# A two-block transformer kernel: the downward products of the second block's MLPs by seven products of halves (Strassen's method)

## The chip, the cores and the metric

The kernel runs on one core of one Trainium2 chip. A core has a matrix engine (TensorE, PE in the profile; PEld is its loading of weights), three engines for elementwise work (VectorE = DVE, ScalarE = ACT, GpSimd = POOL), queues that start transfers (here above all that of SyncE, SPq), an on-chip memory SBUF, and PSUM, into which PE writes its sums. Each engine runs its own list of instructions in order, and waits on semaphores for the others. The metric is the time of one execution on the device, in microseconds (us).

## The reference

Two blocks, one after the other, on 512 tokens of width 1024, in 32-bit floats. The first is an attention block with a mixture of 32 experts; the change does not touch it. The second has two layers, each with a mixer and then an MLP, and the MLP is what is changed:

```python
S, D_MODEL, D_FF = 512, 1024, 4096
def second_block(x, positions, attn_norm_w, w_in, hgrn_lower_bounds, w_out, mlp_norm_w, w_up, w_down, final_norm_w):
    ...
    for layer in range(2):
        ...
        x = x + mixed @ w_out[layer]
        h = rms_norm_2(x, mlp_norm_w[layer])
        x = x + jnp.square(jax.nn.relu(h @ w_up[layer])) @ w_down[layer]
    return rms_norm_2(x, final_norm_w)
```

## The kernel before

Every large product is made of matmuls on numbers split in two: `split` (L83) writes a rounded high part on ACT (L85) and the remainder on DVE (L86), and `mm3` (L88) adds three matmuls, high by high, high by low and low by high (L90 to L92). Each matmul takes a 128x128 stationary operand and up to 512 columns, and writes one PSUM bank of 128x512 numbers.

`mlp` (L1756) works through the hidden width 4096 in four quarters, `b` = 0 to 3. A quarter has an upward part and a downward part.

- Upward: `cols_mm` (L1395) for four pieces of 256 hidden columns each. A piece is one load of 1 MB on the SP queue (`wide`, L1356), one split of 128x2048 numbers (`whi`, `wlo`), and 48 matmuls of 512 columns into two banks of `pa`. Each bank goes through relu and square on ACT and DVE into the high and low parts `uh`, `ul` (L1785 to L1788). In quarter 0 two pieces are done together, first for the first half of the tokens and then for the second, since the last rows of the normed input are still being made; these matmuls have 256 columns.
- Downward: `rows_mm` (L1368) twice, for output columns 0 to 511 and 512 to 1023. Each takes two loads and splits, and for each of four tiles of 128 tokens 24 matmuls into one bank. DVE adds the bank to the residual stream `xs` (`add_rows`, L1410).

Loaded weights lie in `raw`, three buffers of 1 MB. The split weights of the upward part rotate through two buffers, those of the downward part through two others (pools `hi5`, `lo5`). A framework builds the program: it takes the order of each engine's list from priorities and dependences, so that instructions need not stand in the order of the code, and it inserts the semaphores. Around the MLP stand `mix_attention` with the last normalisation (`normed`, L1309, whose rows are scaled by DVE in L1327 and transposed by PE in L1338), and the next layer's mixer or the final norm.

Of the kernel before, what the change touches and what calls it, by code (L numbers as in the profile page):

```python
# [10 lines left out]
F32 = mybir.dt.float32  # L11
F32R = mybir.dt.float32r
# [3 lines left out]
AF = mybir.ActivationFunctionType  # L16
OP = mybir.AluOpType
# [4 lines left out]
P = 128  # L22
S = 512
D = 1024
NT = S // P
KD = D // P
# [43 lines left out]
def bcast_rows(ap, n):  # L70
    return bass.AP(tensor=ap.tensor, offset=ap.offset, ap=[[0, P], [1, n]])


class K:
# [65 lines left out]
    def build(self):  # L140
        tc = self.tc
        with ExitStack() as ctx:
            E = ctx.enter_context
            self.cp = E(tc.tile_pool(name="consts", bufs=1))
            self.dr = E(tc.tile_pool(name="dr", bufs=1, space=DRAM))
            self.sm = E(tc.tile_pool(name="small", bufs=2, reuse_waits="tile"))
            self.xs = self.cp.tile([P, NT, D], F32, name="xs")
            self.raw = E(tc.tile_pool(name="rawp", bufs=3, reuse_waits="tile"))
            self.rawx, self.nraw = None, 0
            with tc.tile_pool(name="cq", bufs=1, side="right", reuse_waits="tile") as self.cq:  # L150
                with tc.tile_pool(name="ps", bufs=1, space=PSUM) as self.ps:
                    self.first_block()
                self.hip = E(tc.tile_pool(name="hip", bufs=2, reuse_waits="tile"))
                self.lop = E(tc.tile_pool(name="lop", bufs=2, reuse_waits="tile"))
# [1599 lines left out]


    def mlp(self, layer, hh, hl):  # L1756
        nc, tc, A, sm, xs = self.nc, self.tc, self.A, self.sm, self.xs
        DVE, ACT, PE = nc.vector, nc.scalar, nc.tensor
        up, down = A["w_up_2"][layer], A["w_down_2"][layer]
        with ExitStack() as c:  # L1760
            E = c.enter_context
            dn = [E(tc.tile_pool(name=n, bufs=2 if n == "hi5" else 2, reuse_waits="tile")) for n in ("hi5", "lo5")]
            pd = E(tc.tile_pool(name="pd3", bufs=1, reuse_waits="tile"))
            h = None
            if layer == 0:
                h, after = self.normed(pd, A["attn_norm_w_2"][1:2])
            else:
                fw = pd.tile([P, D], F32, name="wb")
                nc.gpsimd.dma_start(fw, bcast_rows(A["final_norm_w_2"], D))

                def after(t):
                    ss = sm.tile([P, 1], F32, name="s1")
                    o = pd.tile([P, D], F32, name="xo", bufs=3)
                    ACT.activation(o, xs[:, t, :], AF.Square, accum_out=ss)  # L1774
                    rs = self.rsqrt_mean(sm, ss, D, 1)
                    DVE.scalar_tensor_tensor(o, xs[:, t, :], rs, fw, OP.mult, OP.mult)  # L1776
                    nc.sync.dma_start(self.out[t * P:(t + 1) * P, :], o)
            for b in range(4):
                uh = pd.tile([P, KD, S], F32R, name="uh")
                ul = pd.tile([P, KD, S], F32R, name="ul")  # L1780

                def done(q):
                    def f(j, pt):
                        r = pd.tile([P, S], F32, name="r", bufs=2)
                        ACT.activation(r, pt, AF.Relu)  # L1785
                        ACT.activation(uh[:, 2 * q + j, :], r, AF.Square)
                        DVE.tensor_tensor(r, r, r, OP.mult)
                        DVE.tensor_tensor(ul[:, 2 * q + j, :], r, uh[:, 2 * q + j, :].bitcast(F32), OP.subtract)  # L1788
                    return f
                ps = [(1024 * b + 256 * q, done(q)) for q in range(4)]  # L1790
                if b == 0:
                    self.cols_mm(hh, hl, up, ps[:2], 2)
                    ps = ps[2:]
                for p in ps:
                    self.cols_mm(hh, hl, up, [p])
                self.rows_mm(uh, ul, down, 0, self.add_rows(0), 8 * b, pools=dn)
                last = b == 3
                self.rows_mm(uh, ul, down, 512, self.add_rows(512, after if last else None), 8 * b, by_tile=last, pools=dn)
        return h


# [25 lines left out]
```

## Time and profile before

| | before |
|---|---|
| median of three runs | 2971.6 us (2971.32 to 2974.15) |
| the profiled execution, its own time | 2975.91 us |
| its span, first to last instruction | 2974.1 us |
| PE busy | 2828.0 us (95%) |
| DVE busy | 2143.2 us (72%) |
| ACT busy | 1611.0 us (54%) |
| POOL busy | 286.8 us (10%) |
| MLP of the first layer, about | 1948 to 2298 us |
| MLP of the second layer, about | 2615 to 2965 us |

Busy shares are means over stages with different limits. The records of neighbouring matmuls overlap, so PE's busy time is no measure of its speed; the spacing of the starts is. The profile says which engine's instruction ended an idle stretch, as in `[2.03 <-PE pa L92]`.

### The profile page before, as it was taken

What the parts mean: (1) busy time and instruction counts of PE and PEld (TensorE: products, weight loads), DVE (VectorE), ACT (ScalarE), POOL (GpSimd) and SP (SyncE); (2) the same over time, 40 slices, a digit from 0 to 9 for tenths busy, and PEclk for the clock granted to TensorE, in tenths of its full rate; (3) what the DMA queues carried; (4) which work ended last, traced back from release to release, by engine and by line L of the source; (5) the groups of instructions that cost most, each with busy time, mean ns of one, the idle gap of its engine ahead of it and who ended that gap; (6) DMA issues with size and microseconds to landing.
All of it is one profiled execution on the core that took longest, in us unless ns stands there. A gap on an engine that the chain in (4) does not pass through costs nothing. (4 is left out here: it accounts for less than half of the span.)

```text
span 2974.1 us, 36626 instructions
## 1 busy us (share of the span) xinstructions
PE 2828.0 (95%) x14296; PEld 2122.7 (71%) x14296; DVE 2143.2 (72%) x3043; ACT 1611.0 (54%) x1846; POOL 286.8 (10%) x125
## 2 busy tenths in 40 slices
PE   6988969999999999999997999999999999999998
PEld 4645747666666666666664877788888877788887
DVE  5798679999999999999997586654334586654334
ACT  5478747777777777777775225742223225743222
POOL 1002201122222222222200000000000000000000
PEclk8999969999999999999998999999999999999999
DMA  7244259999999999999996112132322112033330
GB/s 257 83 148 159 89 177 334 363 362 362 358 364 361 360 363 362 360 363 361 362 356 237 57 57 88 29 114 99 99 94 76 57 57 88 29 115 98 99 99 29
DMA packets 184645, 589.38 MB, mean 198 GB/s; under 512 B 16923, under 2 KB 63494, under 8 KB 151702
## 3 DMA queue, kind: packets, MB, share of 16 engines
q1 hardware_dynamic: 174088, 556.81, 51.7%
q0 software_dynamic: 8016, 28.05, 3.8%
q10 hardware_dynamic: 2366, 2.14, 0.3%
q8 instruction: 114, 1.87, 0.3%
q14 instruction: 61, 0.50, 0.0%
HBM read 567.13 MB, written 19.84 MB: 197 GB/s over the span
## 5 line engine op out<-in xcount | busy, mean ns | idle before, releaser
L86 DVE TENSOR_TENSOR wlo<-raw,whi 128x2048 fp32r<-128x2048 f32 (+2 forms) x528 | 1162.6, 2216 | 362.2 <-ACT whi L85 361.4
L85 ACT ACTIVATE whi<-raw 128x2048 fp32r<-128x2048 f32 (+2 forms) x528 | 972.4, 1854 | 579.6 <-PE pa L92 325.2
L90 PE MATMUL pa<-hh,whi 128*128 128x512 f32 (+1 forms) x808 | 289.8, 360 | 0.9 <-ACT whi L85 0.9
L1065 PE MATMUL ph<-whi,xh 128*96 128x512 f32 x1024 | 288.9, 399 | 0.0
L91 PE MATMUL pa<-hl,whi 128*128 128x512 f32 (+1 forms) x808 | 288.9, 358 | 0.0
L1065 PE MATMUL ph<-wlo,xh 128*96 128x512 f32 x1024 | 288.9, 400 | 0.0
L92 PE MATMUL pa<-hh,wlo 128*128 128x512 f32 (+1 forms) x808 | 287.7, 358 | 0.2 <-DVE wlo L86 0.2
L1065 PE MATMUL ph<-whi,xl 128*96 128x512 f32 x1024 | 277.8, 392 | 0.0
L1065 PEld LDWEIGHTS ph<-whi,xl 128*96 128x96 f32 x1024 | 164.7, 161 | 71.4
L1065 PEld LDWEIGHTS ph<-whi,xh 128*96 128x96 f32 x1024 | 161.3, 162 | 63.5 <-issue 0.3
L1065 PEld LDWEIGHTS ph<-wlo,xh 128*96 128x96 f32 x1024 | 159.2, 162 | 62.0 <-DVE wlo L86 0.6
L91 PE MATMUL pa<-wlo,uh 128*128 128x512 f32 x512 | 199.3, 389 | 0.0
L92 PE MATMUL pa<-whi,ul 128*128 128x512 f32 x512 | 199.2, 389 | 0.0
L90 PE MATMUL pa<-whi,uh 128*128 128x512 f32 x512 | 199.0, 389 | 0.0
L989 POOL DMA_INDIRECT xg<-h2d,ig x32 | 146.2, 4570 | 468.3 <-issue 381.3
L1065 PE MATMUL py<-wlo,ah 128*96 128x512 f32 x512 | 161.9, 397 | 14.1 <-DVE wlo L86 14.0
L90 PEld LDWEIGHTS pa<-hh,whi 128*128 128x128 f32 x808 | 153.9, 191 | 25.7 <-ACT z L572 1.8
L92 PEld LDWEIGHTS pa<-hh,wlo 128*128 128x128 f32 x808 | 153.5, 190 | 22.3 <-DVE wlo L86 0.6
L91 PEld LDWEIGHTS pa<-hl,whi 128*128 128x128 f32 x808 | 154.0, 191 | 21.5
L1065 PE MATMUL py<-whi,al 128*96 128x512 f32 x512 | 159.6, 393 | 0.6 <-DVE al L86 0.6
L1065 PE MATMUL py<-whi,ah 128*96 128x512 f32 x512 | 160.1, 394 | 0.0
L90 PE MATMUL pa<-whi,hh 128*128 128x512 f32 (+2 forms) x352 | 135.6, 386 | 1.3 <-ACT hh L273 1.3
(430 smaller groups left out, 4446.4 us busy)
## 6 DMA issues: line engine op xcount, KB each, us to landing
raw<-in_w_mlp SPq DMA_DIRECT2D x384, 1024.0 KB
raw<-in_w_up SPq DMA_DIRECT2D x32, 1024.0 KB
raw<-in_w_down SPq DMA_DIRECT2D x32, 1024.0 KB
raw<-in_w_in SPq DMA_DIRECT2D x26, 1024.0 KB
raw<-in_w_ada SPq DMA_DIRECT2D x24, 1024.0 KB
raw<-in_w_out SPq DMA_DIRECT2D x8, 1024.0 KB
raw<-in_w_o SPq DMA_DIRECT2D x4, 1024.0 KB
acc<-g SPq DMA_DIRECT2D x5, 512.0 KB
```

The costliest lines, as they stand in the source:

```text
L85: nc.scalar.activation(hi, src, AF.Copy)
L86: (engine or nc.vector).tensor_tensor(lo, src, hi.bitcast(F32), OP.subtract)
L90: mm(out, lh, rh, start=start, stop=False)
L91: mm(out, lh, rl, start=False, stop=False)
L92: mm(out, ll, rh, start=False, stop=stop)
L989: POOL.indirect_dma_start(out=xg, out_offset=None, in_=self.h2d[:, :], in_offset=bass.IndirectOffsetOnAxis(ap=ig[:, :1], axis=0))
L1065: PE.matmul(out[:, 512 * n:512 * n + 512], x[:, kk, :], w[:, nn * k + n, :], start=False, stop=kk == KD - 1 and q == 2)
```

## The change

In quarters 0 to 2 of each layer the downward part (512 tokens x 1024 hidden x 1024 outputs) is seen as 2x2 halves: tokens in two halves, outputs in two halves, and the hidden width in two halves of four 128-row blocks (even and odd blocks). Instead of eight products of halves there are seven, in the form of Strassen's method with shared sums. A product has 24 matmuls of 512 columns into two banks. In the code's order, with the weights that each takes (w11, w21, w12, w22 are the loaded quarters of the weight, and t2, w12', w11', w21' sums of them):

1. `first[0]` by w11; 2. `first[1]` by w21; 3. slot 5 by t2; 4. slot 4 by w12'; 5. slot 6 by w11'; 6. slot 7 by w22; 7. slot 2 by w21'.

The sums of weights w12' = w12 - w11, t2 = w22 - w12', w11' = t2 - w11 and w21' = t2 - w21 are GpSimd operations of 128x2048 numbers (L1809, L1810, L1869, L1875); the sums of activations are DVE operations of 128x256 (L1827 to L1831) in tile `s`. Splits are made in halves of 128x1024, weights into four rotating quarters of two `whi` and two `wlo` tiles (`halves`), activations into `ah`, `al`. Results that go to two places are collected in `u` and added to `xs` by GpSimd, 128x1024 at a time (`both`, L1862); the others are added by DVE from PSUM (L1857). Quarter 3 stays with eight products, with the split weights in the same rotating quarters.

```diff
...
+        hi, lo = [[p.tile([P, 4, 512], F32R, name=n) for _ in range(2)] for p, n in ((self.hip, "whi"), (self.lop, "wlo"))]
+        turn = [0]
+        def halves(raw):
+            k, n = raw.shape[1:]
+            out = []
+            for g in range(2):
+                q = turn[0] % 4
+                turn[0] += 1
+                v = [t[q // 2][:, q % 2 * 2:q % 2 * 2 + 2, :].rearrange("p a b -> p (a b)").rearrange("p (k n) -> p k n", n=n) for t in (hi, lo)]
+                self.split(v[0], v[1], raw[:, g * k // 2:(g + 1) * k // 2, :])
+                out += [(v[0][:, q, :], v[1][:, q, :]) for q in range(k // 2)]
...
+            s = pd.tile([P, 4, 8, 256], F32, name="s")
+            own = {n: pd.tile([P, 4, 512], F32, name="w" + n) for n in ("12", "22", "11", "21")}
+            def pieces(b):
+                for nm, k, n in (("12", 0, 1), ("11", 0, 0), ("22", 1, 1), ("21", 1, 0)):
+                    src = down[8 * b * P:8 * (b + 1) * P, 512 * n:512 * n + 512].rearrange("(q two p) n -> p two q n", two=2, p=P)
+                    nc.sync.dma_start(own[nm], src[:, k])
+                t2 = self.rawtile()
+                POOL.tensor_tensor(own["12"], own["12"], own["11"], OP.subtract)
+                POOL.tensor_tensor(t2, own["22"], own["12"], OP.subtract)
+                return t2
...
+                def done(q):
+                    def f(j, pt):
+                        r = pd.tile([P, S], F32, name="r", bufs=2)
+                        ACT.activation(r, pt, AF.Relu)
+                        DVE.tensor_tensor(s[:, q, 2 * j:2 * j + 2, :].rearrange("p a b -> p (a b)"), r, r, OP.mult)
+                        v = [s[:, q, n, :] for n in range(8)]
+                        ACT.activation(first[j][0][:, q, :], v[2 * j + 1], AF.Copy)
+                        if j == 0:
+                            DVE.tensor_tensor(v[6], v[1], v[0], OP.subtract)
+                        else:
+                            DVE.tensor_tensor(v[4], v[0], v[2], OP.add)
+                            DVE.tensor_tensor(v[5], v[2], v[6], OP.subtract)
+                            DVE.tensor_tensor(v[7], v[3], v[5], OP.subtract)
+                        DVE.tensor_tensor(first[j][1][:, q, :], v[2 * j + 1], first[j][0][:, q, :].bitcast(F32), OP.subtract)
+                    return f
+                ps = [(1024 * b + 256 * q, done(q)) for q in range(4)]
+                n = 2 if b == 0 else 1
+                upper(ps[:n], n)
+                t2 = pieces(b)
+                for p in ps[n:]:
+                    upper([p])
+                def parts(slot):
+                    ah, al = left()
+                    self.split(ah, al, s[:, :, slot, :])
+                    return ah, al
+                def product(banks, a, w):
+                    w = halves(w)
+                    for q, (wh, wl) in enumerate(w):
+                        for n in range(2):
+                            ns = slice(n * P, (n + 1) * P)
+                            self.mm3(banks[n], a[0][:, q, ns], a[1][:, q, ns], wh, wl, q == 0, q == 3)
+                def add(banks, half, col, op=OP.add):
+                    for n in range(2):
+                        o = xs[:, 2 * half + n, 512 * col:512 * col + 512]
+                        DVE.tensor_tensor(o, o, banks[n], op)
+                def both(u, half, col):
+                    o = xs[:, 2 * half:2 * half + 2, 512 * col:512 * col + 512]
+                    POOL.tensor_tensor(o, o, u, OP.add)
...
+                u = pd.tile([P, 2, 512], F32, name="u")
+                x = banks(self.pb)
+                product(x, first[0], own["11"])
+                POOL.tensor_tensor(own["11"], t2, own["11"], OP.subtract)
+                for n in range(2):
+                    ACT.copy(u[:, n, :], x[n])
+                both(u, 1, 0)
+                y = banks(self.py)
+                product(y, first[1], own["21"])
+                POOL.tensor_tensor(own["21"], t2, own["21"], OP.subtract)
+                add(y, 1, 0)
+                z = banks(self.pa)
+                product(z, parts(5), t2)
+                for n in range(2):
+                    DVE.tensor_tensor(u[:, n, :], u[:, n, :], z[n], OP.add)
+                both(u, 1, 1)
+                y = banks(self.pa)
+                product(y, parts(4), own["12"])
+                add(y, 1, 1)
+                add(y, 0, 1)
+                x = banks(self.pb)
+                product(x, parts(6), own["11"])
+                for n in range(2):
+                    DVE.tensor_tensor(u[:, n, :], u[:, n, :], x[n], OP.add)
+                both(u, 0, 0)
+                both(u, 0, 1)
+                y = banks(self.py)
+                product(y, parts(7), own["22"])
+                add(y, 1, 1)
+                y = banks(self.pa)
+                product(y, parts(2), own["21"])
+                add(y, 0, 0, OP.subtract)
+            for b in range(3):
+                quarter(b)
...
-                if b == 0:
-                    self.cols_mm(hh, hl, up, ps[:2], 2)
-                    ps = ps[2:]
-                for p in ps:
-                    self.cols_mm(hh, hl, up, [p])
-                self.rows_mm(uh, ul, down, 0, self.add_rows(0), 8 * b, pools=dn)
-                last = b == 3
-                self.rows_mm(uh, ul, down, 512, self.add_rows(512, after if last else None), 8 * b, by_tile=last, pools=dn)
+            for q in range(4):
+                upper([(1024 * b + 256 * q, done(q))])
+            for c0 in (0, 512):
+                finish = self.add_rows(c0, after if c0 else None)
+                pts = [self.pa() for _ in range(NT)]
+                w = []
+                for q in range(2):
+                    w += load(down, 8 * b + 4 * q, c0, 512, 4)
+                    for t in range(NT if c0 == 0 or q else 0):
+                        ts_ = slice(t * P, (t + 1) * P)
+                        for k in range(0 if c0 else 4 * q, 4 * q + 4):
+                            self.mm3(pts[t], uh[:, k, ts_], ul[:, k, ts_], w[k][0], w[k][1], k == 0, k == KD - 1)
+                        if q:
+                            finish(t, pts[t])
```

Three places of the engines' lists follow, as the built programs have them; what stands behind a name is the tile's number.

On ACT, at the start of the first layer's MLP of before: `whi` from `raw_16368` is the high part of quarter 0's third upward piece, `r` and `uh` the relu and square of the first two pieces' four banks (`pa_16152` to `pa_16155`).

```order
L1785 ACTIVATE r_16276<-pa_16152 128x512
L1786 ACTIVATE uh_16138<-r_16276 128x512
L85 ACTIVATE whi_16370<-raw_16368 128x2048
L1785 ACTIVATE r_16305<-pa_16153 128x512
L85 ACTIVATE whi_16560<-raw_16558 128x2048
L1786 ACTIVATE uh_16138<-r_16305 128x512
```

The same place of the change, where `raw_16384` is the third upward piece, `raw_16454` the fourth, `pa_16156` the last of the four banks, and `ah` the high part of an activation sum:

```order
L1822 ACTIVATE r_16307<-pa_16154 128x512
L1825 ACTIVATE ah_16139<-s_16132 128x256
L1822 ACTIVATE r_16339<-pa_16155 128x512
L1825 ACTIVATE ah_16137<-s_16132 128x256
L1822 ACTIVATE r_16369<-pa_16156 128x512
L1825 ACTIVATE ah_16139<-s_16132 128x256
L85 ACTIVATE whi_16125<-raw_16384 128x1024 x2
L85 ACTIVATE whi_16126<-raw_16454 128x1024 x2
```

The third piece's split, which stood behind the first bank's output, now stands behind the last bank's.

On DVE of the change, from the last upward output of quarter 0 to the middle of product 4 (`r_16516` is the last bank's relu, `raw_16381` is t2, `al_16595` and `al_16632` belong to products 3 and 4, `w12_16133` holds w12'):

```order
L1823 TENSOR_TENSOR s_16132<-r_16516 128x512
L1829 TENSOR_TENSOR s_16132<-s_16132 128x256
L1830 TENSOR_TENSOR s_16132<-s_16132 128x256
L1832 TENSOR_TENSOR al_16140<-s_16132,ah_16139 128x256
L1831 TENSOR_TENSOR s_16132<-s_16132 128x256
L86 TENSOR_TENSOR wlo_16127<-raw_16381,whi_16125 128x1024
L86 TENSOR_TENSOR al_16595<-s_16132,ah_16594 128x1024
L86 TENSOR_TENSOR al_16632<-s_16132,ah_16631 128x1024
L86 TENSOR_TENSOR wlo_16127<-raw_16381,whi_16125 128x1024
L86 TENSOR_TENSOR wlo_16128<-w12_16133,whi_16126 128x1024
L1857 TENSOR_TENSOR xs_63<-xs_63,py_16559 128x512
```

All but the last row read two SBUF operands; in before DVE had, in the downward part of a quarter, four splits and eight additions from PSUM.

On POOL of the change, from the first sum of quarter 0 to the second sum of quarter 1 (`w11_16135`, `w21_16136` and `w22_16134` are single buffers that each quarter loads again, `u_16524` the collected results; before had no row here):

```order
L1809 TENSOR_TENSOR w12_16133<-w12_16133,w11_16135 128x2048
L1810 TENSOR_TENSOR raw_16381<-w22_16134,w12_16133 128x2048
L1869 TENSOR_TENSOR w11_16135<-raw_16381,w11_16135 128x2048
L1875 TENSOR_TENSOR w21_16136<-raw_16381,w21_16136 128x2048
L1862 TENSOR_TENSOR xs_63<-xs_63,u_16524 128x2x512 x2
L1809 TENSOR_TENSOR w12_16133<-w12_16133,w11_16135 128x2048
L1862 TENSOR_TENSOR xs_63<-xs_63,u_16524 128x2x512 x2
L1810 TENSOR_TENSOR raw_16855<-w22_16134,w12_16133 128x2048
```

The next quarter's first sum stands between the two pairs of additions of this quarter.

## Rows read from the trace of the kernel before

**Rows 1.** The page: the span, and busy time by engine.

```profile
span 2974.1 us, 36626 instructions
PE 2828.0 (95%) x14296; PEld 2122.7 (71%) x14296; DVE 2143.2 (72%) x3043; ACT 1611.0 (54%) x1846; POOL 286.8 (10%) x125
```

**Rows 2.** Windows: both MLPs, and one downward part; us, busy, clock, DMA.

```profile
1948.00:2298.00 350.00, 349.13 (x1641) 292.36 (x1640) 153.26 (x170) 106.97 (x112) 0.00 (x0) 1.00 0.32 103
1994.00:2037.00 43.00, 43.00 (x191) 35.63 (x190) 15.10 (x13) 8.78 (x6) 0.00 (x0) 1.00 0.30 98
...
2615.00:2965.00 350.00, 349.64 (x1632) 292.80 (x1631) 147.89 (x174) 100.63 (x105) 0.00 (x0) 1.00 0.28 91
```

**Rows 3.** Waits of PE in 1950 to 2298: us, times, longest.

```profile
PE pb L1338 <- DVE xn L1327: 0.4, 1, 0.4
```

**Rows 4.** Timeline of DVE, downward part: additions after 12 matmuls each.

```profile
2119.77 0.69 DVE L1415 TENSOR_TENSOR xs<-xs,pa 128x512 f32<-128x512 f32 x1 [0.60 <-PE pa L92]
2122.49 0.69 DVE L1415 TENSOR_TENSOR xs<-xs,pa 128x512 f32<-128x512 f32 x1 [2.03 <-PE pa L92]
2125.21 0.69 DVE L1415 TENSOR_TENSOR xs<-xs,pa 128x512 f32<-128x512 f32 x1 [2.03 <-PE pa L92]
```

**Rows 5.** Groups of DVE by shape, 1950 to 2298: count, busy us, mean ns.

```profile
L86 DVE TENSOR_TENSOR wlo<-raw,whi 128x2048 fp32r<-128x2048 f32 x33 | 75.6, 2292 | 130.4 <-ACT whi L85 130.4
...
L1787 DVE TENSOR_TENSOR r<-r 128x512 f32<-128x512 f32 x32 | 21.9, 688 | 24.2 <-ACT uh L1786 24.2
```

**Rows 6.** Groups of ACT by shape, 1950 to 2298.

```profile
L1785 ACT ACTIVATE r<-pa 128x512 f32<-128x512 f32 x32 | 18.8, 587 | 42.7 <-PE pa L92 42.0 <-DVE ul L1788 0.7
L1325 ACT ACTIVATE xn<-xs 128x1024 f32<-128x1024 f32 x4 | 4.2, 1060 | 5.9 <-DVE xs L1415 5.9
```

**Rows 7.** Timeline of POOL in the second layer's mixer.

```profile
2473.12 1.29 POOL L1558 TENSOR_TENSOR xn<-uu 128x512 f32<-128x512 f32 x1 [9.22 <-DVE gs L1752]
2474.50 1.34 POOL L1559 TENSOR_TENSOR uu<-uu 128x512 f32<-128x512 f32 x1
2475.92 0.74 POOL L1560 TENSOR_TENSOR uu<-xn 128x256 f32<-128x256 f32 x1
2476.61 2.79 POOL L1561 TENSOR_TENSOR uu<-xn 128x256 f32<-128x256 f32 x1
```

**Rows 8.** Timeline of DVE over the same stretch.

```profile
2472.98 0.69 DVE L1493 TENSOR_TENSOR kd<-pb,kd 64x512 fp32r<-64x512 f32 x1
2473.69 1.01 DVE L1478 TENSOR_TENSOR pt<-pt 128x256 f32<-128x256 f32 x1
2474.73 0.69 DVE L1475 TENSOR_TENSOR pt<-pa,sincos 128x512 f32<-128x512 f32 x1
...
2475.94 2.87 DVE L86 TENSOR_TENSOR wlo<-raw,whi 128x2048 fp32r<-128x2048 f32 x1
...
2479.55 0.43 DVE L1477 TENSOR_TENSOR pt<-pt 128x256 f32<-128x256 f32 x1
2479.89 0.42 DVE L1478 TENSOR_TENSOR pt<-pt 128x256 f32<-128x256 f32 x1
```

**Rows 9.** Timeline of DVE, hand-over from the mixer to the MLP.

```profile
1946.75 2.29 DVE L86 TENSOR_TENSOR wlo<-raw,whi 128x2048 fp32r<-128x2048 f32 x1
...
1954.98 1.28 DVE L1327 SCALAR_TENSOR_TENSOR xn<-xs,rs_y,wb 128x1024 f32<-128x1024 f32 x1
1957.71 0.69 DVE L86 TENSOR_TENSOR hl<-pb,hh 128x512 fp32r<-128x512 f32 x1 [1.45 <-ACT hh L85]
```

**Rows 10.** Timeline of PE: third upward piece of quarter 0 begins.

```profile
1972.66 0.40 PE L90 MATMUL pa<-hh,whi 128*128 128x512 f32 x1
1972.90 0.40 PE L91 MATMUL pa<-hl,whi 128*128 128x512 f32 x1
```

**Rows 11.** Timelines of SP and ACT: a load's issue, and who waited for it.

```profile
1978.15 32.02 SPq L1362 DMA_DIRECT2D raw<-in_w_up  x4
...
1983.84 1.92 ACT L85 ACTIVATE whi<-raw 128x2048 fp32r<-128x2048 f32 x1 [4.25 <-DMA raw<-in_w_up]
```

More of the change, by code (lines that the diff above doesn't have):

```diff
@@ L1757, in mlp @@
         nc, tc, A, sm, xs = self.nc, self.tc, self.A, self.sm, self.xs
-        DVE, ACT, PE = nc.vector, nc.scalar, nc.tensor
+        DVE, ACT, PE, POOL = nc.vector, nc.scalar, nc.tensor, nc.gpsimd
         up, down = A["w_up_2"][layer], A["w_down_2"][layer]
-        with ExitStack() as c:
[L1761 to L1764, printed above, removed]
+        h = None
@@ new lines, in mlp @@
+        hi, lo = [[p.tile([P, 4, 512], F32R, name=n) for _ in range(2)] for p, n in ((self.hip, "whi"), (self.lop, "wlo"))]
[9 more added lines that the diff above has]
+                out += [(v[0][:, q, :], v[1][:, q, :]) for q in range(k // 2)]
+            return out
@@ new lines, in load, with upper @@
+        def load(src, r0, c0, n, nk):
+            raw = self.rawtile().rearrange("p a b -> p (a b)").rearrange("p (k n) -> p k n", k=nk)
+            nc.sync.dma_start(raw, src[r0 * P:(r0 + nk) * P, c0:c0 + n].rearrange("(k p) n -> p k n", p=P))
+            return halves(raw)
+        def upper(ps, parts=1):
+            ws = [load(up, 0, c0, 256, KD) for c0, _ in ps]
+            pts = [[self.pa() for _ in range(2)] for _ in ps]
+            n = S // parts
+            for hf in range(parts):
+                ns = slice(hf * n, hf * n + n)
+                for w, pp, (_, done) in zip(ws, pts, ps):
+                    for j in range(2):
+                        js = slice(j * P, (j + 1) * P)
+                        for k, (wh, wl) in enumerate(w):
+                            self.mm3(pp[j][:, ns], wh[:, js], wl[:, js], hh[:, k, ns], hl[:, k, ns], k == 0, k == KD - 1)
+                        if hf == parts - 1:
+                            done(j, pp[j])
@@ new lines, in mlp, with quarter, left, banks @@
+        with ExitStack() as c:
+            pd = c.enter_context(tc.tile_pool(name="pd3", bufs=1, reuse_waits="tile"))
+            s = pd.tile([P, 4, 8, 256], F32, name="s")
[8 more added lines that the diff above has]
+                return t2
+            def quarter(b):
+                def left():
+                    return [pd.tile([P, 4, 256], F32R, name=n, bufs=3) for n in ("ah", "al")]
+                first = [left() for _ in range(2)]
+                def done(q):
[36 more added lines that the diff above has]
+                    POOL.tensor_tensor(o, o, u, OP.add)
+                def banks(make):
+                    return [make() for _ in range(2)]
+                u = pd.tile([P, 2, 512], F32, name="u")
[32 more added lines that the diff above has]
+                quarter(b)
@@ L1765, in mlp, with tile @@
+        with ExitStack() as c:
+            pd = c.enter_context(tc.tile_pool(name="pd4", bufs=1, reuse_waits="tile"))
+            b = 3
+            uh, ul = [pd.tile([P, KD, S], F32R, name=n) for n in ("uh", "ul")]
+            spare = [pd.tile([P, D], F32, name=f"sp{q}") for q in range(3)]
             if layer == 0:
-                h, after = self.normed(pd, A["attn_norm_w_2"][1:2])
+                class Rows:
+                    def tile(self, shape, dtype, name, bufs=1):
+                        return spare[0] if name == "wb" else spare[1]
+                h, after = self.normed(Rows(), A["attn_norm_w_2"][1:2])
@@ L1767, in mlp @@
             else:
-                fw = pd.tile([P, D], F32, name="wb")
+                fw = spare[0]
                 nc.gpsimd.dma_start(fw, bcast_rows(A["final_norm_w_2"], D))
@@ L1772, in after @@
                     ss = sm.tile([P, 1], F32, name="s1")
-                    o = pd.tile([P, D], F32, name="xo", bufs=3)
+                    o = spare[1 + t % 2]
                     ACT.activation(o, xs[:, t, :], AF.Square, accum_out=ss)
@@ L1777, in after @@
                     nc.sync.dma_start(self.out[t * P:(t + 1) * P, :], o)
[L1778 to L1790, printed above, removed]
-                if b == 0:
-                    self.cols_mm(hh, hl, up, ps[:2], 2)
-                    ps = ps[2:]
-                for p in ps:
-                    self.cols_mm(hh, hl, up, [p])
-                self.rows_mm(uh, ul, down, 0, self.add_rows(0), 8 * b, pools=dn)
-                last = b == 3
-                self.rows_mm(uh, ul, down, 512, self.add_rows(512, after if last else None), 8 * b, by_tile=last, pools=dn)
@@ new lines, in done, with f @@
+            def done(q):
+                def f(j, pt):
+                    r = pd.tile([P, S], F32, name="r", bufs=2)
+                    ACT.activation(r, pt, AF.Relu)
+                    ACT.activation(uh[:, 2 * q + j, :], r, AF.Square)
+                    DVE.tensor_tensor(r, r, r, OP.mult)
+                    DVE.tensor_tensor(ul[:, 2 * q + j, :], r, uh[:, 2 * q + j, :].bitcast(F32), OP.subtract)
+                return f
+            for q in range(4):
+                upper([(1024 * b + 256 * q, done(q))])
```

## The prediction

> **What bounds the kernel now.** I read the page first: PE is busy for 95% of the span [rows 1]. That is a mean over stages, so I then read the two MLPs by themselves, as windows: PE 349 of 350 us, clock 1.00, DVE under half, POOL nothing [rows 2]. Then who PE waits for there: one wait of 0.4 us in the whole MLP [rows 3]. So this stage is set by the number of matmuls, and a matmul that goes is worth its spacing, as long as nobody makes PE wait. The spacing is read where DVE adds finished banks: 2.72 us between additions, 12 matmuls, so 0.2267 us each [rows 4]. A product of 24 matmuls is 5.44 us, half of one 2.72 us.
>
> **What goes.** The downward part of a quarter had 192 matmuls and has seven times 24, 168. Three quarters lose 72 in a layer: 72 x 0.2267 = **16.3 us a layer, 32.6 us in all**. No other matmul changes.
>
> **What comes, and its prices.** ACT takes 1.06 us for 1024 numbers and 0.59 from PSUM for 512 [rows 6]. DVE takes 2.29 us for 2048 and 0.69 for 512 [rows 5], so about 1.22 for 1024, and 0.42 for 256; of independent instructions one starts 0.09 us before the record ahead of it ends (2479.55 and 2479.89) [rows 8]. POOL took 0.74 for 256 and 1.29 for 512 [rows 7], 0.55 more for 256 more; 1024 is then 2.4 us and 2048 about 4.6 us. No row has these lengths: the bounds for 2048 are eight such steps, 4.4, and four rows of 1.34, 5.4. I take 4.6, the straight line through the two rows.
>
> The Trainium skill's page "GPSIMD Engine Reference" (section 3.1, elementwise accounting) gives 4.50 us for this sum of 2048 numbers; by that the total below would be some 2 us lower.
>
> **DVE and POOL do not run beside each other.** This decides the sum. In rows 7 and 8 a DVE instruction with two SBUF operands (L1478, 0.42 us when alone) starts at 2473.69 under a POOL instruction that ends at 2474.41, and takes 1.01 us: it waits that end out. The split at 2475.94 meets POOL's 2475.92 to 2476.66 and takes 2.87 instead of 2.29 us; POOL's next 256 numbers, behind that split, take 2.79 instead of 0.74. L1475, which reads PSUM, ran at its usual 0.69 us under POOL [rows 7, 8]. So a POOL sum and a DVE instruction that reads two SBUF operands take turns, for their whole length, and additions from PSUM are free of it.
>
> The Trainium skill says the same for any length ("SBUF — State Buffer", section "Who interferes with whom"); rows here show it only to 512 numbers on POOL, and the change uses up to 2048.
>
> The load on this shared path in seven products: DVE 14 weight halves and 5 activation parts, 19 x 1.22 = 23.2 us; POOL w21', the next quarter's w12' and four additions, 2 x 4.6 + 4 x 2.4 = 18.8 us; together 42.0 us, while PE needs 38.1. It is over-booked by 4 us, so PE must wait for about that, unless some of it moves into the upward part. I follow the orders to see where. Time 0 is product 1's first matmul.
>
> (a) Product 3. The second half of w21 is split at 0 to 2.3 (1.06 + 1.22), which lets POOL's w21' start: 2.3 to 6.9. DVE still has four 256-wide instructions of the last upward bank, now held until 6.9, done at 8.6; then t2's first half 9.8, the activation parts of products 3 and 4, 11.0 and 12.2. POOL's addition of product 1 has been ready since ACT's copies, about 11, and goes first: 14.6. Then t2's second half, 15.8; with eight starts 0.09 early, 15.1. PE wants it for the 14th matmul of product 3, at 10.88 + 13 x 0.2267 = 13.8. PE waits **1.3 us** (bounds 0 and 2.4, the addition).
>
> (b) Product 5: the second addition stands ahead of the second half of w11'. By the same steps **0.4 us** (0 to 2.4).
>
> (c) Product 7. The next w11 is loaded when DVE has split w11', at about 26.4; a load took 5.7 us from issue to its reader [rows 11], 32.1. POOL's next w12' gets the path when the split in hand ends, 33.2, and holds it to 37.8; the second half of w21' is split by 39.0. PE, 1.7 us late by now, wants it at 32.6 + 1.7 + 3.0 = 37.3: **1.7 us** (0 to 4.6).
>
> (d) POOL's last two additions and the next t2 meet the splits of the next quarter's first upward piece: **1.0 us** (0 to 2.4), a guess between its bounds.
>
> Quarters 0 and 1 lose 4.4 us each; quarter 2 has no next sums and loses (a) and (b), 1.7. A layer: 10.5 us.
>
> (e) Start of a layer. w12' of quarter 0 becomes ready while DVE goes from the mixer to the MLP without a pause (1946.75 to 1956.26) [rows 9]. Its 4.6 us push back the split of the first upward piece. The half split is 1.1 us shorter than the whole one that PE waited for, so I take **3.5 us** (0 to 4.6); the 0.4 us of rows 3 goes.
>
> (f) Third upward piece of quarter 0. It began at 1972.66 [rows 10], its split made ahead of the earlier banks' outputs. Now the split stands on ACT behind the last bank's output: relu 0.59, DVE 0.69, copy 0.4, then 1.06 for the half, and the last matmul's own 0.39 less one spacing: **3.0 us**, and 0.8 more for the low half (1.22 less two matmuls): **3.8 us** (0 not possible by the order; up to 8 if a POOL sum meets it).
>
> Taken at nothing: ACT has 19 x 1.06 + 2 x 0.59 = 21.3 us per 38.1 (cover gone: 1.06 a part). The upward part has on DVE about 25 us of 43.5, and t2 and w11' on POOL, 9.2, fit in the rest (one met badly: 4.6). The four own loads of 1 MB are as many bytes as before, and have the upward part to land in; SP issues the later upward loads behind them, and a piece of slack, 10.9 us, covers 5.7. The last quarter has the same matmuls; its two output buffers instead of three are 5.44 us a tile apart.
>
> **The sum.** A layer: 10.5 + 3.5 - 0.4 + 3.8 - 16.3 = +1.1; two layers +2.2. The profiled execution took 2975.9 us, which makes 2978.1; it stood 4.3 us above the median of the runs, so I predict **2974 us**: the gain is eaten.
>
> **Rivals.** First, the sums hide after all: POOL and DVE find gaps, and (a) to (e) cost nothing. For it: DVE is under half busy in the MLP [rows 2], and each wait is 1 to 2 us, so a little slack removes one. Against it: the path is over-booked by 4 us. Then a layer gains 16.3 + 0.4 - 3.8 = 12.9 us: 2971.6 - 25.8 = 2946 us. Between this and the forecast lies everything in which half the waits vanish, about 2960.
>
> Second, slower: POOL's long sums cost four short ones, 5.4 and 2.7 us. Then (a) grows by 1.1, (b) by 0.3, (c) by 0.8, (d) by 0.3 in a full quarter, (a) and (b) in the third, (e) by 0.8: 2 x 2.5 + 1.4 + 0.8 = 7.2 a layer, 14.4 in all: 2988 us. For it: the trace has no long POOL instruction. Against it: 256 to 512 numbers cost less than double. It decides from 4.8 us a sum (about 1.8 us a layer for 0.2 us more).
>
> Third, the path's turns: if DVE always went ahead of a waiting POOL, (d) and the additions in (a) and (b) would go, but what waits for POOL's results (DVE's additions to xs, in order) would come late instead: a gain of up to 3 a layer, 2968 us.
>
> **Chances.** This kernel's runs differ by 0.1%; 0.2%, 6 us, is what a measurement can tell from no change. The forecast with the third rival, 2966 to 2977: 0.42. The sums hidden in part or wholly, below 2966: 0.31, of which 0.10 below 2950. The long POOL sums, above 2977: 0.27, of which 0.10 above 2988. Leaving out both tails of 0.10 the range is 2950 to 2988; the likeliest case alone is 2966 to 2977.
>
> **What would show it.** Right: PE waits in products 3 and 7 of each quarter, released by DVE's wlo, with the DVE instruction ahead stretched and ending with a POOL record; POOL sums of 4.6 us; a wait of 3 us at the third upward piece, released by ACT's whi. Wrong: DVE splits of 1.22 us beside running POOL sums; PE without a gap over 0.3 us in a quarter; POOL records over 5 us with no DVE split under them; or a spacing other than 0.2267 within a product.

## The result, and the profile after

The changed kernel takes 2990.5 us (median of 4 runs, 2989.0 to 2993.1) against 2971.5 us: ratio 1.0063, 95% interval 1.0051 to 1.0074. It is 19 us slower; 2974 was forecast, with 2988 as the upper end of the range. Of all the runs in this document one is left out of its median: a run of `filled_on_dve` that took 8434 us.

The page of the changed kernel, against [rows 1]:

```profile
span 2988.9 us, 36965 instructions
PE 2811.2 (94%) x14152; PEld 2101.8 (70%) x14152; DVE 2389.6 (80%) x3305; ACT 1681.3 (56%) x1988; POOL 487.9 (16%) x173
```

144 matmuls are gone, worth 32.6 us by their spacing, and yet the span is 14.8 us longer. (The medians differ by 19 us: the profiled execution of before stood 4.3 us above the median that the forecast started from, that of the change at its own.) The waits of PE in the first layer, 1950 to 2298 (us in total, times, longest), against the single wait of [rows 3]:

```profile
PE pa L91 <- DVE wlo L86: 8.5, 5, 2.8
PE pa L92 <- DVE wlo L86: 4.4, 3, 3.5
PE pa L90 <- ACT whi L85: 2.9, 1, 2.9
PE pb L91 <- DVE wlo L86: 0.7, 3, 0.3
```

16.5 us in twelve waits, all but 2.9 us for the low half of a split, where 0.4 us was. Where such a wait comes from is seen at product 7 of quarter 0, on the timeline of POOL and then of DVE:

```profile
2036.75 5.36 POOL L1809 TENSOR_TENSOR w<-w,w 128x2048 f32<-128x2048 f32 x1 [5.96 <-DMA w<-in_w_down]
...
2036.45 1.21 DVE L86 TENSOR_TENSOR al<-s,ah 128x1024 fp32r<-128x1024 f32 x1
2037.59 5.60 DVE L86 TENSOR_TENSOR wlo<-w,whi 128x1024 fp32r<-128x1024 f32 x1
```

POOL's sum meets a DVE split, and the split after that takes 5.60 us instead of 1.2: it ends 1.08 us after POOL does. On PE, in the same place:

```profile
2040.03 0.39 PE L90 MATMUL pa<-whi,ah 128*128 128x512 f32 x1
2043.24 0.56 PE L91 MATMUL pa<-wlo,ah 128*128 128x512 f32 x1 [2.82 <-DVE wlo L86]
...
2044.02 0.63 PE L90 MATMUL pa<-whi,ah 128*128 128x512 f32 x1
2044.45 0.63 PE L91 MATMUL pa<-wlo,ah 128*128 128x512 f32 x1
...
2047.46 0.39 PE L90 MATMUL pa<-whi,ah 128*128 128x512 f32 x1
2047.69 0.39 PE L91 MATMUL pa<-wlo,ah 128*128 128x512 f32 x1
```

Two things are to be seen: the wait of 2.8 us, and that the matmuls behind it start 0.43 us apart, and only from about 2047 on 0.23 again. Windows of the first layer (length, busy time of PE, PEld, DVE, ACT and POOL, granted clock, DMA) show the same at three places; a granted clock of 1.00 is 2.4 GHz, 0.50 is 1.2 GHz. Before, it was 1.00 throughout [rows 2]:

```profile
1952.00:1956.00 4.00, 1.72 (x10) 1.73 (x11) 4.00 (x5) 0.00 (x0) 1.13 (x1) 0.85 0.00 0
1956.00:1960.00 4.00, 4.00 (x27) 4.00 (x27) 3.79 (x13) 0.00 (x0) 0.00 (x0) 0.72 0.00 0
...
1980.00:1984.00 4.00, 2.73 (x7) 1.92 (x8) 4.00 (x6) 3.53 (x4) 0.00 (x0) 0.76 0.00 0
1984.00:1988.00 4.00, 4.00 (x16) 3.22 (x15) 1.35 (x2) 0.00 (x0) 0.00 (x0) 0.81 0.88 259
...
2040.00:2044.00 4.00, 1.18 (x4) 0.63 (x3) 4.00 (x3) 1.06 (x1) 2.11 (x1) 0.94 0.14 55
2044.00:2048.00 4.00, 4.00 (x13) 3.17 (x12) 4.00 (x3) 0.00 (x0) 3.54 (x2) 0.63 0.33 86
```

Each of the three lies behind a wait of about 3 us or more: the start of the layer, the third upward piece of quarter 0, and product 7. What the clock was short of 1.00, times 4 us and summed over the six rows, is 0.60 + 1.12 + 0.96 + 0.76 + 0.24 + 1.48 = 5.2 us.

### The profile page after: what moved, and what is told of

It reads as the page before. It is cut to its first block, busy times and chain, and to the rows that moved or that the text cites. A ratio compares the mean times of both kernels' runs of the same rounds, so it can differ in the third digit from the quotient of the medians.

```text
span 2988.9 us, 36965 instructions
## 1 busy us (share of the span) xinstructions
PE 2811.2 (94%) x14152; PEld 2101.8 (70%) x14152; DVE 2389.6 (80%) x3305; ACT 1681.3 (56%) x1988; POOL 487.9 (16%) x173
## 4 chain that ended last, share of the span: by engine, by line
PE 65%; DVE 23%; issue 6%; ACT 4%; DMA 2%; another core or an unknown queue 0%; SPq 0%; DVEq 0%; ACTq 0%
PE ph L1065 16%; DVE wlo L86 11%; PE pa L92 9%; PE pa L90 9%; PE pa L91 9%; PE py L1065 8%; PE yp L497 2%; ACT whi L85 1%; PE pt L482 1%; PE ph L1055 1%; DVE s L1829 1%; PE ho L1742 1%; DVE al L86 1%; PE b L1013 1%; DVE gl L1022 1%
## 5 line engine op out<-in xcount | busy, mean ns | idle before, releaser
L85 ACT ACTIVATE whi<-raw 128x2048 fp32r<-128x2048 f32 (+2 forms) x556 | 945.2, 1714 | 367.9 <-PE pa L92 119.2
L1186 POOL DMA_INDIRECT acc<-yo,isc x31 | 79.1, 2550 | 558.5 <-ACT yo L1185 558.5
L91 PE MATMUL pa<-wlo,hh 128*128 128x512 f32 (+2 forms) x352 | 132.0, 375 | 4.0 <-DVE wlo L86 4.0
L92 PE MATMUL pa<-whi,hl 128*128 128x512 f32 (+2 forms) x352 | 131.3, 375 | 0.0
```

The source lines that it names most:

```text
L85: nc.scalar.activation(hi, src, AF.Copy)
L91: mm(out, lh, rl, start=False, stop=False)
L92: mm(out, ll, rh, start=False, stop=stop)
L1186: POOL.indirect_dma_start(out=self.acc[:, :], out_offset=bass.IndirectOffsetOnAxis(ap=s["isc"][:, :1], axis=0), in_=yo, in_offset=None, co ...
```

## The experiments

**Theory:** a POOL sum and DVE's instructions with two SBUF operands take turns; PE waits for the DVE splits that are held up; and behind a wait of about 3 us the granted clock falls to 0.5 (1.2 GHz) for a while, which costs 1.7 us or 3.4 us more. **Rivals:** the waits come from the halved splits and from the order of ACT's and DVE's lists; products wait because POOL's sums are late; the falls of the clock have nothing to do with the waits.

The runs are set out by the whole time (the last four columns), and by the length of each layer in the profiled execution, from the start of DVE's last but one addition in the mixer (L1534) to the start of its last in the MLP (L1415; in before 1944.50 to 2302.13). Ratios are to runs of before on the same chip, whose medians were 2970.8 to 2974.3 us. Earlier stages, which no edit touches, differ by up to 9 us between profiled executions; the layers are free of that.

| run | layer 0 | layer 1 | median | lowest | highest | ratio, 95% interval |
|---|---|---|---|---|---|---|
| before | 357.63 | 355.47 | 2971.5 | 2969.2 | 2974.2 | |
| changed | 365.38 | 362.55 | 2990.5 | 2989.0 | 2993.1 | 1.0063 (1.0051 to 1.0074) |
| `sums_on_dve` | 349.69 | 345.81 | 2954.9 | 2953.6 | 2956.3 | 0.9942 (0.9925 to 0.9958) |
| `no_sums` | 340.47 | 337.72 | 2940.1 | 2934.9 | 2941.8 | 0.9884 (0.9868 to 0.9901) |
| `third_piece_early` | 363.55 | 361.12 | 2980.5 | 2976.6 | 2983.6 | 1.0027 (1.0017 to 1.0036) |
| `filled_waits` | 366.44 | 365.16 | 2991.4 | 2988.0 | 2995.8 | 1.0064 (1.0047 to 1.0080) |
| `dve_sums_early_piece` | 343.03 | 340.23 | 2943.3 | 2942.1 | 2945.1 | 0.9901 (0.9884 to 0.9917) |
| `after_again` | 369.75 | 365.21 | 2991.0 | 2986.9 | 2996.7 | 1.0054 (1.0038 to 1.0071) |
| `unread_sums` | 372.34 | 369.71 | 3005.1 | 3002.0 | 3011.0 | 1.0113 (1.0096 to 1.0130) |
| `weights_on_dve` | 358.61 | 355.85 | 2973.1 | 2971.1 | 2976.6 | 1.0002 (0.9992 to 1.0012) |
| `unread_copies` | 347.07 | 344.83 | 2953.4 | 2950.8 | 2956.4 | 0.9938 (0.9919 to 0.9957) |
| `filled_on_dve_2` | 347.04 | 344.35 | 2949.9 | 2948.6 | 2953.4 | 0.9925 (0.9908 to 0.9941) |

**All sums on DVE** (`sums_on_dve`; the five calls in `pieces`, `both` and `quarter`):

```diff
-                POOL.tensor_tensor(own["12"], own["12"], own["11"], OP.subtract)
+                DVE.tensor_tensor(own["12"], own["12"], own["11"], OP.subtract)
...
```

> The five kinds of sums that POOL made in the MLPs (w12', t2, w11', w21' and the additions of u) are made by DVE, in the same places of the code; nothing else changes. Theory (DVE and POOL take turns, and a sum holds the path 4.6 to 5.6 us on POOL but 2.29 on DVE): in seven products DVE has 19 x 1.22 + 2 x 2.29 + 4 x 1.22 = 32.6 us against PE's 38.1, so the waits inside the products go, and with the first sum behind the first splits the one at the start goes too. Left is the third upward piece, 3.4 us of wait and 1.7 us of clock a layer: 2971.5 - 2 x (16.7 - 5.1) = 2948 us, up to 2955 if 1 us a quarter stays. Rival (the waits come from halved splits and the order of ACT's and DVE's lists): DVE only gets more to do, 2990 to 2996 us.

2954.9 us, the upper end of what the theory gave and far from the rival. Of the waits inside a quarter's products 0.8 us is left; the third piece waits 3.3 us a layer.

**No sums** (`no_sums`; all `POOL.tensor_tensor` and `both` lines go, and product 3 takes `own["22"]`):

```diff
-                t2 = self.rawtile()
-                POOL.tensor_tensor(own["12"], own["12"], own["11"], OP.subtract)
...
-                product(z, parts(5), t2)
+                product(z, parts(5), own["22"])
...
```

> All sums of weights and the additions of u are left out (the products take the loaded weights as they are, so the result is not the reference's); all halved splits, products and bank additions stay. Theory: no POOL instruction is left, so only the third upward piece waits: 2948 us, within 3 us of the run with the sums on DVE. Rival (halved splits and order): the waits in products 3 and 7 stay, 2980 to 2990 us.

2940.1 us, lower than either expected, and 31 to 32 us below before: nearly the whole 32.6 us (34.9 us by the two layers, in which before's own short waits are gone too). Its waits in the first layer:

```profile
PE pa L92 <- DVE wlo L86: 0.6, 1, 0.6
PE pb L1338 <- DVE sp L1327: 0.4, 1, 0.4
```

So the halved splits and seven products cost nothing by themselves; the first rival falls for the waits inside the products. The third piece's wait is gone too, which was not expected: without `t2` in a `raw` buffer the framework puts that piece's splits between the outputs of the first four banks. Every run that keeps `t2` in `raw` and the split where it was has a gap of 2.9 to 3.3 us there in both layers (unless it is filled), whether POOL or DVE makes the sums or POOL only copies. So that wait comes from the place of the split in ACT's list, as the next run shows, and that place goes with `t2` in `raw`.

**The third piece's split ahead of the outputs** (`third_piece_early`, in `upper`):

```diff
...
+                    if hf == parts - 1 and early:
+                        if w is ws[0]:
+                            ahead.append(load(up, 0, early, 256, KD))
+                        for j in range(2):
+                            done(j, pp[j])
...
```

> The load and split of quarter 0's third upward piece stand ahead of the first two pieces' outputs, as the before kernel's list had it; POOL's sums stay. Theory: the wait of 2.9 + 0.5 us goes and with it the stretch at half clock behind it, 1.7 us: 5.1 us a layer, 2990.5 - 10.2 = 2980 us. Rival (the wait is only moved on to the first products of the quarter, since DVE and POOL are over-booked there): 2986 to 2990 us.

2980.5 us, as the theory had it, 10 us below the changed kernel; but the trace supports it only in part. The wait and its fall are gone: from the last output of the second piece to that of the fourth, layer 0 takes 5.5 us less. A part of that is given back: the start of layer 0 waits 4.3 us now, at the transposes (L1338), and product 7 waits 3.0 us in three quarters instead of two, with 1.2 GHz behind each of these. The layers are 3.3 us shorter than those of the changed kernel's first profiled execution, 10.3 us shorter than those of its second (`after_again`).

**The waits filled with matmuls** (`filled_waits`):

```diff
...
+            if c0 == 512:
+                for _ in range(12):
+                    PE.matmul(pts[0][0], hh[:, 0, :P], hh[:, 0, :], start=True, stop=True)
...
+                if b == 0 and layer == 0:
+                    for _ in range(12):
+                        PE.matmul(y[0], hh[:, 0, :P], hh[:, 0, :], start=True, stop=True)
```

> Four of PE's waits are filled with matmuls whose result nobody reads: 28 of 256 columns at the start of layer 0, 12 of 512 columns ahead of the third upward piece in both layers and 12 ahead of product 7 of quarter 0 in layer 0; 64 matmuls more, nothing less. Theory (the granted clock falls to 0.5 because of the wait ahead of it, and costs 1.7 us each time): the granted clock stays at 1.00 in layer 0 and at the third piece of layer 1, and the kernel gains 4 x 1.7 = 6.8 us although it does more: 2983.7 us. Rival (the falls have nothing to do with the waits): clock as before, 2990 us or up to 2 us more.

2991.4 us: by its time the rival. By its rows the three places that were filled (third piece twice, product 7 once) have a granted clock of 1.00. But the fill at the start of layer 0 missed its wait: ten of its matmuls ran ahead of a wait of 4.3 us at the transposes and eighteen behind it, where they took 3.9 us of PE's time (1951.07 to 1954.98) that the kernel's own matmuls could have had. And in layer 1, product 7 of quarters 0 and 1, where nothing was filled, waited 3.0 us twice with 1.2 GHz behind. A kernel whose waits of product 7 differ from one execution to the next can't tell theory and rival apart by its time; hence the run on DVE below.

**Both edits together** (`dve_sums_early_piece`: `third_piece_early` with all sums on DVE)

> Both edits together: all sums on DVE, and the third upward piece's split ahead of the first outputs. Theory: the run with the sums on DVE had two waits left that are longer than 1 us, 3.3 us at the third piece of each layer, each with 1.7 to 3.4 us at half clock behind it; without them 2954.9 - 2 x 5.6 = 2943 to 2945 us, near the 2940 us of the run without sums. Rival (the order only moves the wait: DVE's sum of w12' now stands ahead of the third piece's splits): 2951 to 2955 us.

2943.3 us, as the theory had it: 28 to 30 us faster than before, 47 faster than the changed kernel, and 3 us from the run without sums. Its waits in the first layer, 1940 to 2298:

```profile
PE pa L91 <- DVE wlo L86: 1.7, 3, 0.6
PE pa L92 <- DVE wlo L86: 0.5, 1, 0.5
PE pb L1338 <- DVE sp L1327: 0.3, 1, 0.3
```

**The changed kernel once more** (`after_again`)

> The changed kernel once more, unaltered, as a yardstick for the others of this call. Theory and rival alike: 2990 us within 4, and waits of 16 to 18 us a layer; if it comes near 2981, the 10 us by which the run with the early third piece stood below it were not that edit's.

2991.0 us. The profiled execution is one of the long ones: its waits of product 7 are 2.1 to 3.0 us in four quarters instead of 1.4 to 3.0, each with 1.2 GHz behind it. That is the spread of this kernel.

**Sums that nobody reads** (`unread_sums`; the additions of `u` are left out):

```diff
-                POOL.tensor_tensor(own["12"], own["12"], own["11"], OP.subtract)
+                POOL.tensor_tensor(t2, own["12"], own["11"], OP.subtract)
                 POOL.tensor_tensor(t2, own["22"], own["12"], OP.subtract)
...
-                POOL.tensor_tensor(own["11"], t2, own["11"], OP.subtract)
+                POOL.tensor_tensor(dead, v4(own["22"]), v4(own["11"]), OP.subtract)
...
```

> POOL makes the four sums of weights of each quarter, each as long as before, but nobody reads them: the products take the loaded weights (the result is not the reference's); the additions of u are left out. So a sum that comes late can make nobody wait; only the path between POOL and DVE is left. Theory (DVE is held for the length of a sum): the start of a layer still waits 3.5 us with 1.7 at half clock behind it, product 7 still waits 1.4 to 3 us in two quarters, and the third piece, whose order is unchanged, 3.4 + 1.7: 2940 + 2 x (5.2 + 3 + 5.1) = 2966 us. Rival (products wait for late sums): only the third piece is left, 2940 + 10.2 = 2950 us.

3005.1 us, slower than the changed kernel, although no product waits for a sum. The rival of late sums falls; the theory's 2966 us is missed by 39. The timelines of POOL, DVE and PE at products 1 to 3 of quarter 0:

```profile
2005.82 4.63 POOL L1873 TENSOR_TENSOR s<-w,w 128x2048 f32<-128x2048 f32 x1 [38.27 <-DVE s L1828]
2010.52 4.65 POOL L1878 TENSOR_TENSOR s<-w,w 128x2048 f32<-128x2048 f32 x1
...
2005.85 4.87 DVE L1831 TENSOR_TENSOR al<-s,ah 128x256 fp32r<-128x256 f32 x1
2010.65 4.81 DVE L1830 TENSOR_TENSOR s<-s 128x256 f32<-128x256 f32 x1
...
2016.65 0.79 PE L91 MATMUL pa<-wlo,ah 128*128 128x512 f32 x1 [3.13 <-DVE wlo L86]
```

Two DVE instructions that take 0.42 us by themselves take 4.87 and 4.81, each ending 0.3 us after a POOL sum. Nothing stood between these two sums here, so they came back to back, and product 3 waits 3.3 us and then 0.9 instead of 1.6 in each of the three quarters of both layers, with 1.2 GHz behind it each time. That is why the run is slower than expected.

**Weights on DVE, additions on POOL** (`weights_on_dve`: the four calls on `own` and `t2` moved, `both` not)

> The four sums of weights on DVE, the four additions of u stay on POOL. Theory (any POOL sum holds DVE): DVE's 19 x 1.22 + 2 x 2.29 = 27.8 us and POOL's four additions of 3.3 us as measured, 13.2, make 41 us on a path for which PE leaves 38.1, so the waits in products 3 and 5 stay, 2 us a quarter, while the start and product 7 are free: 2954.9 + 6 x 2 = 2967 us. Rival (only the long sums of weights do harm): 2955 us, as with all sums on DVE.

2973.1 us, 6 us above the theory's figure and 18 above the rival's. The harm is real but in another place: products 3 and 5 wait 0.3 us at most, and the next quarter's first upward piece waits 3.0 us. On DVE and POOL there:

```profile
2031.53 7.67 POOL L1862 TENSOR_TENSOR xs<-xs,u 128x1024 f32<-128x1024 f32 x2 [9.29 <-DVE u L1889]
...
2032.51 4.48 DVE L1809 TENSOR_TENSOR w<-w,w 128x2048 f32<-128x2048 f32 x1
2036.92 3.37 DVE L86 TENSOR_TENSOR wlo<-raw,whi 128x1024 fp32r<-128x1024 f32 x1
```

Two short additions on POOL hold a DVE sum (2.29 us alone) and the split behind it. The expectation counted time twice: an addition's 3.3 us on POOL contains its wait for the DVE split ahead of it. In the changed kernel the one of 2016.09 ends at 2019.36, 2.27 us after the split that it met (2014.74 to 2017.09). With 4 x 2.27 = 9.1 us the path has 36.9 us of work, less than 38.1, and products 3 and 5 fit; the wait is where the turns meet, not where the load is.

**Copies that nobody reads** (`unread_copies`: `POOL.tensor_copy` of one operand in place of each unread sum)

> As the run with the unread sums, but POOL copies 2048 numbers (one operand read) where it made a sum of two operands; nobody reads the copies either, and the result is not the reference's. Theory in its narrow form (POOL and DVE take turns only where two operands are read): DVE's splits keep their 1.2 us beside the copies, and only the third piece waits: 2940 + 2 x 6 = 2952 us. Rival (any POOL instruction on SBUF of this length holds DVE): 3000 us, as with the unread sums.

2953.4 us, as the narrow theory had it, but by luck: its reason is refuted, and what the rival says of a POOL instruction is right in kind. POOL and DVE in quarter 0:

```profile
2002.49 1.90 POOL L1873 COPY s<-w 128x2048 f32<-128x2048 f32 x1 [40.01 <-DVE s L1828]
2004.45 1.97 POOL L1878 COPY s<-w 128x2048 f32<-128x2048 f32 x1
...
2002.54 2.12 DVE L1831 TENSOR_TENSOR al<-s,ah 128x256 fp32r<-128x256 f32 x1
2004.59 2.12 DVE L1830 TENSOR_TENSOR s<-s 128x256 f32<-128x256 f32 x1
```

DVE is held by a copy as well, for its 1.9 us instead of 4.6; that is short enough for PE not to wait in the products. The Trainium skill's page "SBUF — State Buffer" (section "Who interferes with whom") says that a DVE instruction with two SBUF inputs contends with a GpSimd instruction that reads SBUF; the rows agree, 2.12 us for 0.42.

**The wait on DVE filled** (`filled_on_dve` and `filled_on_dve_2`, the same kernel: `sums_on_dve` and 14 matmuls at the third piece)

```diff
+            if ps[0][0] == 512:
+                for _ in range(14):
+                    PE.matmul(pts[0][0], hh[:, 0, :P], hh[:, 0, :], start=True, stop=True)
```

> The kernel with all sums on DVE, whose waits do not depend on POOL's turns; its wait of 3.3 us ahead of the third upward piece is filled, in both layers, with 14 matmuls of 512 columns that nobody reads (14 x 0.2267 = 3.2 us). Nothing is taken away. Theory (the granted clock falls because of the wait): no stretch at 0.5 behind the third piece; there were 6.8 us of it in layer 0 and 3.4 in layer 1, so layer 0 gets 3.4 us shorter and layer 1 1.7: 2954.9 - 5.1 = 2950 us. Rival (the falls come whether PE waits or not): the same stretches at 0.5, both layers as long as they were or longer, 2955 to 2956 us.

> The kernel with all sums on DVE and 14 unread matmuls in the wait ahead of the third upward piece of both layers once more, for its trace, since the profiled execution of the first go was disturbed and shows nothing of these waits. Theory: no wait and no stretch at 0.5 at the third piece; from the second last row that DVE adds in the mixer to the last row of the MLP, layer 0 takes 349.7 - 3.4 = 346.3 us and layer 1 345.8 - 1.7 = 344.1 us, the whole 2950 us. Rival (the falls come whether PE waits or not): the stretches at 0.5 as before, 349.7 and 345.8 us or more, 2955 us.

The first gave 2951.5 us (median of four runs; ratio 0.9929, 0.9911 to 0.9948), the second 2949.9, against 2954.9: 28 matmuls more, and 3 to 5 us less. Windows of `sums_on_dve` and then of `filled_on_dve_2` at the third piece of layer 0 (which begins 3 us earlier in the second):

```profile
1966.00:1970.00 4.00, 0.98 (x9) 0.77 (x7) 3.97 (x8) 2.23 (x4) 0.00 (x0) 0.93 0.00 0
1970.00:1974.00 4.00, 3.61 (x8) 2.40 (x9) 4.00 (x6) 2.99 (x4) 0.00 (x0) 0.50 0.04 10
1974.00:1978.00 4.00, 4.00 (x15) 3.17 (x14) 0.97 (x1) 0.00 (x0) 0.00 (x0) 0.72 0.84 252
```

```profile
1965.00:1969.00 4.00, 4.00 (x24) 3.50 (x23) 3.96 (x8) 2.00 (x4) 0.00 (x0) 1.00 0.00 0
1969.00:1973.00 4.00, 3.75 (x15) 2.47 (x14) 4.00 (x6) 3.24 (x4) 0.00 (x0) 1.00 0.00 0
1973.00:1977.00 4.00, 4.00 (x19) 3.31 (x18) 1.34 (x3) 0.60 (x1) 0.00 (x0) 1.00 0.88 262
```

0.50 and 0.72 became 1.00, layer 0 is 2.65 us shorter and layer 1 1.46 (3.4 and 1.7 expected). The rival of unrelated falls is gone for this place: PE's wait takes the clock down, and matmuls that nobody reads keep it up. For product 7 the one filled quarter above says the same; at the start of a layer no fill met its wait, but in `sums_on_dve` and `no_sums`, where that wait is gone, the fall is gone too.

## Why the prediction was wrong

**What goes** was right: the run without sums got 31 to 32 of the 32.6 us.

**The path of DVE and POOL** was right, also for the lengths of which no row existed: POOL's sum of 2048 alone takes 4.61 to 4.65 us (4.6 forecast), its addition of 1024 takes 2.27 us behind the split that it met (2.4 forecast). Records of 5 us and more have a DVE instruction with two SBUF operands under their beginning, as 2036.75 shows. So the second rival, sums of 5.4 us, came near the measured time with its 2988 us by luck, for a reason that the rows refute.

**The waits** of the changed kernel's first profiled execution, as gaps between starts of neighbouring matmuls less the 0.23 spacing:

| term | forecast | layer 0 | layer 1 |
|---|---|---|---|
| (a) product 3, each quarter | 1.3 | 1.6 | 1.6 |
| (b) product 5, each quarter | 0.4 | 0.5 | 0.5 |
| (c) product 7 with (d) next piece, quarters 0, 1 | 2.7 | 3.0, 2.4 | 2.4, 3.6 |
| (e) start | 3.5 | 3.6 | 4.4 |
| (f) third piece | 3.8 | 3.4 | 3.4 |
| sum of the layer | 17.8 | 18.8 | 20.1 |

The terms were mis-sized by 1.0 and 2.3 us. (c) stood one split earlier than forecast, at the first half of w21'. In layer 1 (e) hit the scaling ahead of the transposes (L1327) instead of the first split. The parts that the forecast names for (f) add up to 2.9 us where it wrote 3.0; the wait for ACT's `whi` there was 2.9.

**The step that failed** is the one from waits to time: the sum took a wait at its own length, and the matmuls behind it at 0.2267 us, the clock of [rows 2]. A spacing other than that within a product was the last of its own signs of being wrong, and product 7 shows 0.43 us. Five of that execution's six waits of 2.9 us and more had a stretch at 1.2 GHz behind them, together 5.2 us by the windows in layer 0, and 5.1 in layer 1 (0.66 over ten us and 0.79 over eight, in part while PE still waited). Before had a wait of 0.4 and 0.5 us at the start of its two layers (the one of [rows 3], at the end of layer 0, has two of 0.3 us in its place). Layer 0: 18.8 - 0.4 + 5.2 - 16.3 = 7.3 us, measured 7.75 (365.38 - 357.63). Layer 1: 20.1 - 0.5 + 5.1 - 16.3 = 8.4, or 7.6 without the 0.8 us of clock that was lost while PE still waited (0.77 from 2622 to 2625.39); measured 7.1. The two measured sums, 14.8 us, are the whole difference of the spans. Of the 12.6 us by which they exceed the forecast's 2.2, about 9.5 are the clock and the rest are the mis-sized waits. The other 4 us between the medians are not explained: there is one trace of before, and it stands above its median.

In the chances, the wait as a cause of a slower clock was no case at all, and every case for slower went through longer sums.

**Left open:** what decides between 1.4 and 3 us at product 7 from one execution to the next was not tried by itself; the rows show only that the sum of w12' starts when its load lands, and so meets another DVE instruction each time.

## What to carry to other kernels

Moving elementwise work to an idle engine is no gain where that engine, while it runs, holds up another for which the busiest one waits: here the same sums took half as long on DVE and made PE wait less, 2954.9 us against 2990.5, though DVE had more to do. Where PE never waits, price a wait of 3 us by its length and by the matmuls behind it at half clock, and look which splits stand in an in-order list behind the results of PE itself. Once both were mended (all sums on DVE, the split early), seven products did pay: 28 to 30 of the 32.6 us. A new tile in a rotating set of buffers can change the order that a framework makes at a place that no line of the edit names.

## What the runs showed of the hardware that was not expected

- In the profiled executions of these kernels 42 gaps of 2.9 to 4.4 us stood in the MLPs, and 41 had a stretch at 1.2 GHz behind them; of 31 gaps of 1.4 to 2.4 us, one had (2.1 us). The exception among the long ones is product 7 of quarter 1 in layer 1 of the changed kernel, 3.0 us; the rows don't show why.
- A copy of 2048 numbers on POOL takes 1.90 us, a sum 4.63 us; the copy holds DVE's two-operand instructions just as the sum does.
- An instruction of 128x256 on DVE (0.42 us alone) can be held for the length of a whole POOL sum, 4.87 us.
